# A two-layer hybrid trunk on one core: the order of weight parts in six blocks, the mean ahead of the root, the sines a block later, one last store

## The chip, the cores and the metric

The kernel runs on one core of one Trainium2 chip. The metric is the device time of that core in microseconds (us). Three timed runs of the kernel before gave 876.5, 876.67 and 876.76 us; their median, 876.67, is the time that is compared. The trace comes from one more execution, which took 876.84 us.

## What is computed

Two layers act on a stream `x` of 256 tokens by 1024 features, in float32; then comes a final RMSNorm. In words of the reference:

```python
def hybrid_layer(x, ...):
    h = rmsnorm(x, norm_mix)
    cb, cc, cu, q, k, v, g, ga, gb = jnp.split(h @ w_in, ...)
    y_conv = short_conv_mixer(cb, cc, cu, conv_w, w_conv_out)          # gated width-3 convolution
    y_ret = retention_mixer(q, k, v, g, positions, ret_norm, w_ret_out)  # rotary q, k; 4 heads
    x = x + (sigmoid(ga) * y_conv + sigmoid(gb) * y_ret) @ w_o
    h2 = rmsnorm(x, norm_mlp)
    return x + square(relu(h2 @ w_up)) @ w_down                        # 1024 -> 4096 -> 1024
```

The weights, some 80 million bytes a layer, are read once from device memory.

## The kernel before

**Numbers in two parts.** A float32 weight is not multiplied as such. ACT rounds it to fp32r (the high part) and DVE subtracts that from the weight (the low part): `split`, lines 104 to 106. Activations are split in the same way. A product is then taken from three of the four part products: high weight with high and low activation, low weight with high activation.

**Blocks.** The weights lie in memory as 152 blocks of 1024 x 256 numbers (76 a layer), each loaded in two halves by SP's queue into `raw` (five half buffers) and split into `parts` (three block buffers). A block of `proj` has 16 steps (8 tiles of the contraction by 2 output tiles). Before the change each step is two matmuls with weights of their own: the high part against both parts of the activation (512 columns), then the low part against the high activation (256 columns). So a block is 32 matmuls, with a weight load for each. Blocks 0 to 3 of a layer (the values `v`) and the last down projection go another way, with the tokens as the stationary side and 512 columns in every matmul.

**The order.** There is no scheduler: every engine runs its instructions in the order in which the Python code writes them. `window` counts the blocks (`cnt`). For block i it first writes the work that was put off with `at(n, fn, ph=...)` (n blocks later; `ph` -1, 0, 1 and 2 stand before, between and after the two halves' splits), with the splits of block i + 2 among it, then the matmuls of block i, then the load of block i + 3, then small products (`products_at`). A block's result leaves PSUM in `collect`: ACT copies one half, DVE adds the other.

**The names that the steps below touch.** In layer 0, `proj` blocks 4 and 5 are the first two of the gate `g`; in each layer blocks 23 and 24 of the layer's 76 (23 and 24, 99 and 100 counted over both) are the last of `g` and the first of `ga`. Around these, `mix_values` (tile `o_ps`) and `head_sums` (`var_ps`) put small products between the blocks. `norm_total` sums the squares of x over the features on PE (`mix_st`, right after block 5 in layer 0), `factors_begin` makes the factor `rr` = 1/sqrt(mean + eps) from it: `rsqrt_begin` (ACT's first guess into `rr`, DVE's mean into `rs_m`), then two steps of `newton` in the next two windows. POOL needs `rr` for the gates. `sines` (ACT) takes the rotary angles' sines, and `rotation_tables` (POOL) makes `sin_t` and `cos_t` of them, which DVE multiplies by `rr` (`cosr`, `sinr`).

**The end.** The last tokens' second half of the output is scaled by DVE in two pieces of 256 columns, each stored from SP's queue, while ACT scales and stores the first half.

Of the kernel before, what the change touches and what calls it, by code (L numbers as in the profile page):

```python
# [16 lines left out]
ALU = mybir.AluOpType  # L17
# [4 lines left out]
KT = D // P  # L22
# [3 lines left out]
EPS = 1e-6  # L26
# [8 lines left out]
def _conv(i):  # L35
    return [(n, o + 256 * i) for n, o in (("cc", 1024), ("cu", 2048), ("cb", 0))]


IN_ORDER = (
    [("g", G0), ("g", G0 + 256)]  # L40
    + _conv(0)
    + [e for qk, c in zip((("q", Q0), ("q", Q0 + 256), ("k", K0)), _conv(1)) for e in (qk, c)]
    + [("k", K0 + 256)]
    + _conv(2) + _conv(3)
    + [("g", G0 + 512), ("g", G0 + 768)]
    + [("ga", GA0 + 256 * i) for i in range(4)]
    + [("gb", GB0 + 256 * i) for i in range(4)]
# [6 lines left out]
def trunk_kernel(ctx, tc, px, pos, w, mask, gf, out):  # L54
    nc = tc.nc
# [28 lines left out]
    def stile(name):  # L84
        return s8.tile([P, KT, T], F32, tag="s8", name=name)

    class Parts:
# [5 lines left out]
        def at(self, k):  # L93
            return self.tiles[k // (KT // 2)][:, k % (KT // 2)]
# [33 lines left out]
    cnt = [0]  # L128
    work, small_products, amid = {}, {}, {}
# [5 lines left out]
    def products_at(n, fn, *args):  # L135
        small_products.setdefault(cnt[0] + n, []).append((fn, args))
# [16 lines left out]
    def window(products):  # L153
        i = cnt[0]
        todo = work.setdefault(i, [])

        def run(ph):

            for e in todo:
                if e[0] == ph:  # L160
                    e[1](*e[2])

        run(-1)
        if i in EAGER:
            split_half(i + 2, 0)
        run(0)
        if i > 2 and i not in EAGER:
            split_half(i + 2, 0)
        run(1)
        if i > 2:  # L170
            split_half(i + 2, 1)
        run(2)
        products(blocks[i])
        load_block(i + 3)
        raws.pop(i), blocks.pop(i)
        for fn, args in small_products.pop(i, []):
            fn(*args)
        cnt[0] += 1

    def mm(o, a, b, start, stop):  # L180
        nc.tensor.matmul(o, lhsT=a, rhs=b, start=start, stop=stop, skip_group_check=True)  # L181

    def proj(act, n_blocks=1):

        ps = ps_main.tile([P, 2, 2, T], F32, tag="mm", name="ps")

        def products(blk, b):  # L190
            for k in range(KT):
                a = act[b].at(k)
                for j in range(2):
                    first, end = b == 0 and k == 0, b == n_blocks - 1 and k == KT - 1
                    mm(ps[:, j], blk[:, 0, 2 * k + j, :], a, first, False)
                    mm(ps[:, j, 1], blk[:, 1, 2 * k + j, :], a[:, 0], False, end)
                    for fn, args in amid.pop((cnt[0], 2 * k + j), []):
                        fn(*args)

        for b in range(n_blocks):  # L200
            window(lambda blk: products(blk, b))
        return ps
# [28 lines left out]
    def collect(ps, t=None):  # L231

        t = t2("sum", "sum", 4) if t is None else t
        nc.scalar.copy(t, ps[:, :, 1, :])  # L234
        nc.vector.tensor_tensor(out=t, in0=ps[:, :, 0, :], in1=t, op=ALU.add)  # L235
        return t
# [6 lines left out]

    def rsqrt_begin(y, m, v, scale):

        nc.scalar.activation(y, v, AF.Abs_reciprocal_sqrt, scale=scale, bias=eps)
        nc.vector.tensor_scalar(out=m, in0=v, scalar1=scale, scalar2=EPS, op0=ALU.mult, op1=ALU.add)

    def column_sums(o, hi, lo):

# [45 lines left out]
    def gains(layer, at, n=KT):  # L296
        o = layer * PER_LAYER + at
        return par_sb[:, o:o + n]
# [39 lines left out]
    for n in range(2):  # L338
        c = slice(4 * n, 4 * n + 4)
# [9 lines left out]
    def first_parts(norm=norm):  # L349

        def parts(i, *ks):
            for n, k in enumerate(ks):
                norm.split(k)
                split_half(i, n)

        at(0, parts, 1, 2, 3)
        at(1, parts, 2, 4, 5)
        at(2, parts, 3, 6, 7)
        at(3, norm.split, 0)
        for i, half in ((4, 0), (4, 1)):  # L360
            at(3, split_half, i, half)
        for p in range(NPAIR):
            at(3 if p < 3 else 4, norm.square, p)
        at(4, norm.fold)
        at(5, norm.split_sum)
# [37 lines left out]
    for layer in range(DEPTH):  # L403
        act = [norm.act]
# [3 lines left out]
        def factors_begin(norm=norm):  # L408
            rs_m, rs_a = (tmp.tile([P, T], F32, tag="tmp1", bufs=7, name=n) for n in ("rs_m", "rs_a"))
            rsqrt_begin(rr, rs_m, norm.total_ps, 1.0 / D)  # L410
            at(1, newton, rr, rs_a, rs_m, ph=-1)
            at(2, factors_end, rs_m, rs_a, ph=-1)
# [17 lines left out]
        if layer == 0:  # L430
            first_parts()
            at(0, reduce_angles)
            at(5, sines, ph=2)
            at(6, rotation_tables)
            at(9, nc.sync.dma_start, mask_sb, mask)
        if layer == 0:
            products_at(5, norm_total)
# [73 lines left out]
        def conv_u(p, ps_u, z):  # L511
            t = collect(ps_u)
            nc.gpsimd.tensor_tensor(out=z, in0=z, in1=both(rr2), op=ALU.mult)
            nc.gpsimd.tensor_tensor(out=z, in0=t, in1=z, op=ALU.mult)
            at(1, conv_in, p, z)
# [80 lines left out]
        def head_out(h, rs):  # L596
# [4 lines left out]
            nc.gpsimd.tensor_tensor(out=y, in0=y, in1=both(rs), op=ALU.mult)  # L601
            at(1, split, y, *yr.pair(h))

        hg = small.tile([P, KT], F32, tag="hg", bufs=2, name="hg")
        nc.gpsimd.tensor_scalar(out=hg, in0=gains(layer, G_RET), scalar1=0.5, scalar2=None, op0=ALU.mult)
        v_ps = proj_tokens(act[0], xs if layer == 0 else None)
# [5 lines left out]
        for name, _ in IN_ORDER:  # L612
            n = seen[name] = seen.get(name, -1) + 1
            if name == "q" and n == 0:
                qk = stile("qk")
                q_parts = s8.tile([P, 2, HEADS, T], F32R, tag="s8", name="q_parts")
                k0_parts = s4.tile([P, 2, HEADS, P], F32R, tag="s4", name="k0_parts")
            elif name == "cc" and n == 0:
                yc = Parts("yc")
            elif name == "cc" and n == 2:  # L620
                sc0_parts = s8.tile([P, 2, HEADS, T], F32R, tag="s8", name="sc0_parts")
                sc1 = s4.tile([P, HEADS, P], F32, tag="s2", bufs=1, name="sc1")
                for h in range(HEADS):
                    products_at(1 + h, scores, h)
            elif name == "g" and n == 2:
                osq = s8.tile([P, 2, HEADS, T], F32R, tag="s8", name="osq")
                for h, later in enumerate((0, 0, 1, 2)):
                    products_at(later, mix_values, h)
                products_at(2, head_sums, 0)
                products_at(4, head_sums, 1)  # L630
            elif name == "ga" and n == 0:
                ta = stile("ta")
            elif name == "gb" and n == 0:
                tb = stile("tb")
            ps = proj(act)
            if name == "q":
                at(0, rotate, n, ps)
                if n == 1:
                    at(1, rotations_of_k, ph=1)
            elif name == "k":  # L640
                at(0, rotate, n + 2, ps)
            elif name == "g":
                at(0, gate, n, ps, 3 if n < 2 else 0)
            elif name == "cc":
                at(0, lambda ps: new("z", collect(ps)), ps)
            elif name == "cu":
                at(0, lambda n, ps: conv_u(n, ps, kept["z"]), n, ps)
            elif name == "cb":
                at(0, conv_b, n, ps)
            elif name == "ga":  # L650
                at(0, merge_gate, ta, n, ps)
            elif name == "gb":
                at(0, merge_gate, tb, n, ps)
# [30 lines left out]
        for p in range(NPAIR):  # L684
            at(0, merge_conv, p, proj([yc]))
        mg = Parts("mg")
        for p in range(NPAIR):
            at(0, merge_ret if p < NPAIR - 1 else merge_last, p, proj([yr]))
# [70 lines left out]
    ps = [[both_ps[:, c] for c in HALVES], [third[:, HALVES[0]], ps_misc.tile([P, 512], F32, tag="misc", name="ps")]]  # L759
# [53 lines left out]
    def scaled(j, n, c, r):  # L813

        f = slice(512 * n + c.start, 512 * n + c.stop)
        nc.vector.scalar_tensor_tensor(
            out=o[j][:, f], in0=ps[j][n][:, c], scalar=r, in1=gain[:, f], op0=ALU.mult, op1=ALU.mult
        )
        nc.sync.dma_start(out=out[tok[j], f], in_=o[j][:, f])
# [19 lines left out]
    c = HALVES[0]  # L839
# [2 lines left out]
    nc.vector.tensor_tensor(out=o[1][:, c], in0=ps[1][0], in1=gain[:, c], op=ALU.mult)  # L842
    squares(1, 1)
    r = root(1)
    for n in range(2):
        scaled(1, 1, slice(256 * n, 256 * n + 256), r)
    nc.scalar.activation(o[1][:, c], o[1][:, c], AF.Copy, scale=r)
    nc.scalar.dma_start(out=out[tok[1], c], in_=o[1][:, c])

# [73 lines left out]
```

## Time and profile before

| what | value |
|---|---|
| median of three runs | 876.67 us |
| the profiled execution | 876.84 us |
| its span, first to last instruction | 875.0 us |
| time outside the span | 1.84 us |
| PE busy | 866.8 us, 99% |
| PE's weight loads busy | 754.1 us, 86% |
| DVE, ACT, POOL busy | 680.2, 529.5, 308.4 us |
| granted TensorE clock | 0.999 of the full 2.4 GHz |

The span is cut by what PE does: its matmuls follow one another from 1 us to the last 6 us. A matmul's duration in the trace runs on into the next one's, so the rate of PE is read from start to start, or from stretches of the chain of waits, not from the mean of one. What the other engines do counts where PE waits for it, and in the last 6 us.

### The profile page before, as it was taken

To read this page: it belongs to the slowest core of one execution; us is meant where nothing else is said; L and a number is where in the kernel's file an instruction comes from. 1 tells how busy PE (TensorE), PEld (TensorE's weight loads), DVE (VectorE), ACT (ScalarE), POOL (GpSimd) and SP (SyncE) were. 2 spreads that over 40 slices of the span, in tenths; PEclk is the share of its full clock that TensorE was granted. 3 is DMA by queue.
4 is the path that set the end of the run, shared out by engine and by line. 5 is a ranking of instruction groups with operands and counts; after the bars stand their busy time and mean duration, and the time that the engine had idled before them with its cause. 6 is when DMAs were issued, how large, how long until landed. Compare 5 with 4: busy or idle time off the path is not lost.

```text
span 875.0 us, 12663 instructions
## 1 busy us (share of the span) xinstructions
PE 866.8 (99%) x4846; PEld 754.1 (86%) x4846; DVE 680.2 (78%) x739; ACT 529.5 (61%) x761; POOL 308.4 (35%) x191
## 2 busy tenths in 40 slices
PE   9999999999999999999999999999999999999997
PEld 6888888888888888888888888888888888888885
DVE  5799899999898766555567989999979896663443
ACT  6766665956467777444447665578645587772333
POOL 3857755361213222000013587455411322240000
PEclk9999999999999999999999999999999999999999
DMA  9746455556655655555554555545565565565541
GB/s 329 231 170 208 138 194 183 168 174 226 202 194 170 216 187 193 196 188 187 178 199 167 183 172 195 171 158 187 185 210 175 194 198 189 191 218 171 196 137 48
DMA packets 45996, 163.53 MB, mean 187 GB/s; under 512 B 5104, under 2 KB 5744, under 8 KB 45936
## 3 DMA queue, kind: packets, MB, share of 16 engines
q1 hardware_dynamic: 45648, 162.29, 55.4%
q8 instruction: 38, 0.62, 0.3%
q10 hardware_dynamic: 288, 0.44, 0.2%
q14 instruction: 22, 0.18, 0.1%
HBM read 161.66 MB, written 1.05 MB: 186 GB/s over the span
## 4 chain that ended last, share of the span: by engine, by line
PE 87%; POOL 5%; DVE 4%; DMA 1%; ACT 1%; issue 1%; SPq 0%; DVEq 0%; POOLq 0%
PE ps L181 85%; DVE parts L106 2%; PE o_ps L181 1%; DMA pos_i<-pos 1%; POOL red L371 1%; POOL ang L386 1%; DMA raw<-w 1%; POOL mix_sum L281 1%; POOL rot L458 1%; POOL qk L459 0%; DVE sum L235 0%; PE sc_ps L181 0%; ACT parts L105 0%; POOL qk L451 0%; POOL acc L534 0%
## 5 line engine op out<-in xcount | busy, mean ns | idle before, releaser
L106 DVE TENSOR_TENSOR parts<-raw,parts 128x1024 fp32r<-128x1024 f32 (+1 forms) x304 | 436.7, 1474 | 94.2 <-ACT parts L105 93.8
L105 ACT CAST parts<-raw 128x1024 fp32r<-128x1024 f32 (+1 forms) x304 | 304.5, 1049 | 110.8 <-PE ps L181 79.8
L181 PE MATMUL ps<-mix,parts 128*128 128x512 f32 (+1 forms) x1792 | 316.1, 337 | 1.0 <-DVE parts L106 1.0
L181 PEld LDWEIGHTS ps<-mix,parts 128*128 128x128 f32 x1792 | 274.0, 188 | 38.9 <-DVE parts L106 1.6
L181 PE MATMUL ps<-mlp,parts 128*128 128x512 f32 (+1 forms) x1024 | 178.1, 336 | 0.0
L181 PEld LDWEIGHTS ps<-mlp,parts 128*128 128x128 f32 x1024 | 156.5, 188 | 20.9
L730 POOL TENSOR_TENSOR u<-u,rr2m 128x512 f32<-128x512 f32 x32 | 46.5, 1454 | 126.2 <-ACT u L729 113.1
L235 DVE TENSOR_TENSOR sum<-ps,sum 128x512 f32<-128x512 f32 x78 | 53.3, 684 | 47.4 <-ACT sum L234 47.3
L181 PE MATMUL ps<-up,parts 128*128 128x512 f32 (+1 forms) x512 | 88.9, 336 | 0.0
L181 PE MATMUL ps<-parts,up 128*128 128x512 f32 x384 | 87.5, 389 | 0.0
L181 PEld LDWEIGHTS ps<-up,parts 128*128 128x128 f32 x512 | 78.3, 188 | 10.5
L181 PEld LDWEIGHTS ps<-parts,up 128*128 128x128 f32 x384 | 71.9, 188 | 14.9
L234 ACT COPY sum<-ps 128x512 f32<-128x512 f32 x78 | 45.4, 583 | 61.9 <-PE ps L181 61.7
L181 PE MATMUL ps<-yr,parts 128*128 128x512 f32 (+1 forms) x256 | 44.7, 336 | 0.0
L181 PE MATMUL ps<-mg,parts 128*128 128x512 f32 (+1 forms) x256 | 44.7, 336 | 0.0
L181 PE MATMUL ps<-yc,parts 128*128 128x512 f32 (+1 forms) x256 | 44.7, 336 | 0.0
L181 PEld LDWEIGHTS ps<-yc,parts 128*128 128x128 f32 x256 | 39.1, 188 | 5.2
L181 PEld LDWEIGHTS ps<-yr,parts 128*128 128x128 f32 x256 | 39.1, 188 | 5.2
L181 PEld LDWEIGHTS ps<-mg,parts 128*128 128x128 f32 x256 | 39.1, 188 | 5.2
L181 PE MATMUL ps<-parts,mix 128*128 128x512 f32 x180 | 41.6, 392 | 0.0
L181 PEld LDWEIGHTS ps<-parts,mix 128*128 128x128 f32 x180 | 33.7, 188 | 7.5 <-ACT parts L105 0.6
L281 POOL TENSOR_TENSOR mix_sum<-mix_sum,sq 128x512 f32<-128x512 f32 x6 | 9.9, 1644 | 83.4 <-ACT sq L279 83.2
(166 smaller groups left out, 747.5 us busy)
## 6 DMA issues: line engine op xcount, KB each, us to landing
raw<-w SPq DMA_DIRECT2D x302, 512.0 KB, 4.0
raw<-w SPq DMA_DIRECT2D x4, 256.0 KB, 5.0
px_sb<-px SPq DMA_DIRECT2D x3, 256.0 KB, 7.3
mask_sb<-mask SPq DMA_DIRECT2D x1, 512.0 KB, 7.6
gain<-gf SPq DMA_DIRECT2D x1, 512.0 KB, 4.5
out<-o SPq DMA_DIRECT2D x2, 256.0 KB, 2.1
out<-o SPq DMA_DIRECT2D x2, 128.0 KB, 2.0
out<-o ACTq DMA_DIRECT2D x1, 256.0 KB, 2.2
```

Of the source, the lines that this page charges most:

```text
L105: nc.scalar.copy(hi, src)
L106: nc.vector.tensor_tensor(out=lo, in0=src, in1=hi.bitcast(F32), op=ALU.subtract)
L181: nc.tensor.matmul(o, lhsT=a, rhs=b, start=start, stop=stop, skip_group_check=True)
L234: nc.scalar.copy(t, ps[:, :, 1, :])
L235: nc.vector.tensor_tensor(out=t, in0=ps[:, :, 0, :], in1=t, op=ALU.add)
L281: nc.gpsimd.tensor_tensor(out=self.sum, in0=self.sum, in1=sq, op=ALU.add)
L371: nc.gpsimd.tensor_scalar(out=out, in0=x_, scalar1=c0, op0=ALU.mult, **ops)
L386: nc.gpsimd.tensor_tensor(out=ang, in0=ang, in1=red, op=ALU.subtract)
L458: nc.gpsimd.tensor_tensor(out=w_, in0=w_, in1=both(sinr), op=ALU.mult)
L730: nc.gpsimd.tensor_tensor(out=u, in0=u, in1=both(rr2), op=ALU.mult)
```

## The change

Four edits. (1) `proj` gets a flag `apart`: with it a block's 16 high matmuls come first, all in a row, and then its 16 low ones; blocks 4 and 5 of layer 0 and blocks 23 and 24 of both layers have it. The sums are the same, in another order. (2) In `rsqrt_begin` DVE's mean is written ahead of ACT's root; both read the same PSUM tile, and the second of them waits for the first. It is used once a layer for the norm and twice a layer for the heads. (3) `sines` moves from window 5 to window 6 (still behind the splits), `rotation_tables` from 6 to 7. (4) The last 512 columns are scaled and stored in one piece.

```diff
-    def proj(act, n_blocks=1):
+    def proj(act, n_blocks=1, apart=False):
...
         def products(blk, b):
-            for k in range(KT):
-                a = act[b].at(k)
-                for j in range(2):
-                    first, end = b == 0 and k == 0, b == n_blocks - 1 and k == KT - 1
-                    mm(ps[:, j], blk[:, 0, 2 * k + j, :], a, first, False)
-                    mm(ps[:, j, 1], blk[:, 1, 2 * k + j, :], a[:, 0], False, end)
...
+            kj = [(k, j) for k in range(KT) for j in range(2)]
+
+            def high(k, j):
+                mm(ps[:, j], blk[:, 0, 2 * k + j, :], act[b].at(k), b == 0 and k == 0, False)
+
+            def low(k, j):
+                mm(ps[:, j, 1], blk[:, 1, 2 * k + j, :], act[b].at(k)[:, 0], False, b == n_blocks - 1 and k == KT - 1)
+
+            if apart:
+                for e in kj:
+                    high(*e)
+                for e in kj:
+                    low(*e)
+                return
...
     def rsqrt_begin(y, m, v, scale):
+        nc.vector.tensor_scalar(out=m, in0=v, scalar1=scale, scalar2=EPS, op0=ALU.mult, op1=ALU.add)
         nc.scalar.activation(y, v, AF.Abs_reciprocal_sqrt, scale=scale, bias=eps)
-        nc.vector.tensor_scalar(out=m, in0=v, scalar1=scale, scalar2=EPS, op0=ALU.mult, op1=ALU.add)
...
-            at(5, sines, ph=2)
-            at(6, rotation_tables)
+            at(6, sines, ph=2)
+            at(7, rotation_tables)
...
+        PER, APART = len(IN_ORDER) + 4 + 12 + 32, (23, 24) + ((4, 5) if layer == 0 else ())
...
-            ps = proj(act)
+            ps = proj(act, apart=cnt[0] % PER in APART)
...
-    for n in range(2):
-        scaled(1, 1, slice(256 * n, 256 * n + 256), r)
+    scaled(1, 1, c, r)
```

On PE, from the end of layer 0's value blocks into block 4, before (`mix_103` and `mix_104` hold the parts of the normed x, `parts` the weights'):

```order
L181 MATMUL ps<-parts,mix_104 128x512 x48
L181 MATMUL ps<-mix_103,parts 128x512
L181 MATMUL ps<-mix_103,parts 128x256
L181 MATMUL ps<-mix_103,parts 128x512
L181 MATMUL ps<-mix_103,parts 128x256
```

The same place after, through blocks 4 and 5 to the column sums:

```order
L181 MATMUL ps<-parts,mix_104 128x512 x48
L181 MATMUL ps<-mix_103,parts 128x512 x8
L181 MATMUL ps<-mix_104,parts 128x512 x8
L181 MATMUL ps<-mix_103,parts 128x256 x8
L181 MATMUL ps<-mix_104,parts 128x256 x8
L181 MATMUL ps<-mix_103,parts 128x512 x8
L181 MATMUL ps<-mix_104,parts 128x512 x8
L181 MATMUL ps<-mix_103,parts 128x256 x8
L181 MATMUL ps<-mix_104,parts 128x256 x8
L181 MATMUL mix_st<-mix_sh,ones 128x256
```

The alternation of 512 and 256 columns has become runs of 16 and 16.

On ACT, behind the last split of window 5 in layer 0, before (`sh` and `turns` are the sines, `rr` the first guess of the root, `rs_a` the square in the Newton step):

```order
L105 CAST parts<-raw 128x1024 [waits DMAHW7_49]
L391 ACT_TABLE_LOAD
L391 ACTIVATE sh<-ang 128x256
L392 ACTIVATE turns<-ang 128x256
L393 ACTIVATE turns<-turns,quarter_turn 128x256 [waits Activation_49]
L246 ACT_TABLE_LOAD
L246 ACTIVATE rr<-mix_st,eps 128x256 [waits PE_49]
L481 ACTIVATE v_parts<-vt,mu 128x256 [waits DVE_49]
```

and after:

```order
L105 CAST parts<-raw 128x1024 [waits DMAHW7_49]
L258 ACT_TABLE_LOAD
L258 ACTIVATE rr<-mix_st,eps 128x256 [waits DVE_49]
L492 ACTIVATE v_parts<-vt,mu 128x256 [waits Activation_49] x2
L245 COPY sg<-ps 128x512 [waits PE_49]
L105 CAST parts<-raw 128x1024 [waits DMAHW0_49]
L105 CAST parts<-raw 128x1024 [waits DMAHW1_49]
L402 ACT_TABLE_LOAD
L402 ACTIVATE sh<-ang 128x256
L403 ACTIVATE turns<-ang 128x256
L404 ACTIVATE turns<-turns,quarter_turn 128x256 [waits Activation_49]
L251 ACTIVATE rs_a<-rr 128x256
```

The three sines and their table load have moved from ahead of the root to behind the next two casts, ahead of the first Newton square; the root now waits for DVE instead of PE.

On DVE at the same place, before:

```order
L106 TENSOR_TENSOR parts<-raw,parts 128x1024 [waits DMAHW7_49,Activation_49]
L247 TENSOR_SCALAR rs_m<-mix_st 128x256 [waits Activation_49]
L487 SCALAR_TENSOR_TENSOR v_parts<-vt,mu,v_parts 128x256 [waits Activation_49] x2
L235 TENSOR_TENSOR sg<-ps,sg 128x512 [waits PE_49,Activation_49]
L106 TENSOR_TENSOR parts<-raw,parts 128x1024 [waits DMAHW0_49,Activation_49]
```

and after:

```order
L106 TENSOR_TENSOR parts<-raw,parts 128x1024 [waits DMAHW7_49,Activation_49]
L257 TENSOR_SCALAR rs_m<-mix_st 128x256 [waits PE_49]
L498 SCALAR_TENSOR_TENSOR v_parts<-vt,mu,v_parts 128x256 [waits DVE_49,Activation_49]
L498 SCALAR_TENSOR_TENSOR v_parts<-vt,mu,v_parts 128x256 [waits Activation_49]
L246 TENSOR_TENSOR sg<-ps,sg 128x512 [waits Activation_49]
```

No row has moved on DVE here; the mean `rs_m` waits for PE's sums instead of ACT's root.

## Rows read from the trace of the kernel before

**Rows 1.** The page: span, then busy time and share of PE and its loads.
```profile
span 875.0 us, 12663 instructions
PE 866.8 (99%) x4846; PEld 754.1 (86%) x4846; DVE 680.2 (78%) x739; ACT 529.5 (61%) x761; POOL 308.4 (35%) x191
```

**Rows 2.** Chain that ended last, in order of time: start, us, engine, tile, instructions.
```profile
126.31 11.10 PE ps L181 x64
...
139.72 5.66 PE ps L181 x32
...
569.48 5.66 PE ps L181 x32
```

**Rows 3.** Timeline of PE, 27 to 40 us: start, us, operation, count.
```profile
27.56 11.45 PE L181 MATMUL ps<-mix,parts 128*128 128x512 f32 x64
38.85 0.28 PE L181 MATMUL mix_st<-mix_sh,ones 128*128 128x256 f32 x1
38.97 0.29 PE L181 MATMUL mix_st<-mix_sl,ones 128*128 128x256 f32 x1
```

**Rows 4.** Groups by form: count, busy us, mean ns of one.
```profile
L181 PE MATMUL ps<-parts,up 128*128 128x512 f32 x384 | 87.5, 389 | 0.0
L181 PEld LDWEIGHTS ps<-yc,parts 128*128 128x128 f32 x256 | 39.1, 188 | 5.2
```

**Rows 5.** Timeline of PE, 859 to 872 us, matmuls of 512 columns alone.
```profile
858.78 10.36 PE L181 MATMUL ps<-parts,up 128*128 128x512 f32 x45
```

**Rows 6.** Timeline of PE, 94 to 120 us: the two waits; in brackets, idle time and releaser.
```profile
95.60 3.74 PE L181 MATMUL ps<-mix,parts 128*128 128x256 f32 x20 [0.64 <-DVE parts L106]
...
107.89 5.59 PE L181 MATMUL ps<-mix,parts 128*128 128x256 f32 x31 [0.34 <-DVE parts L106]
```

**Rows 7.** Timeline of ACT, 39 to 48 us.
```profile
39.99 1.28 ACT L391 ACT_TABLE_LOAD   x1
...
42.57 1.28 ACT L246 ACT_TABLE_LOAD   x1
43.87 0.47 ACT L246 ACTIVATE rr<-mix_st,eps 128x256 f32<-128x256 f32 x1
...
47.41 0.41 ACT L240 ACTIVATE rs_a<-rr 128x256 f32<-128x256 f32 x1
```

**Rows 8.** Timeline of DVE, 40 to 58 us.
```profile
40.01 1.23 DVE L106 TENSOR_TENSOR parts<-raw,parts 128x1024 fp32r<-128x1024 f32 x1 [0.21 <-ACT parts L105]
44.38 0.42 DVE L247 TENSOR_SCALAR rs_m<-mix_st 128x256 f32<-128x256 f32 x1 [3.14 <-ACT rr L246]
...
46.59 2.58 DVE L106 TENSOR_TENSOR parts<-raw,parts 128x1024 fp32r<-128x1024 f32 x2 [0.19 <-ACT parts L105]
49.09 0.41 DVE L241 SCALAR_TENSOR_TENSOR rs_a<-rs_a,rs_m 128x256 f32<-128x256 f32 x1
...
56.24 1.51 DVE L424 TENSOR_TENSOR cosr<-cos_t,rr 128x256 f32<-128x256 f32 x1
```

**Rows 9.** Timeline of POOL, 42 to 58 us.
```profile
42.64 0.74 POOL L397 TENSOR_TENSOR sin_t<-sh,turns 128x256 f32<-128x256 f32 x1 [3.26 <-ACT turns L393]
...
44.37 0.61 POOL L400 TENSOR_TENSOR cos_t<-sh 128x256 f32<-128x256 f32 x1
45.08 0.45 POOL L371 TENSOR_SCALAR cos_t<-cos_t 128x256 f32<-128x256 f32 x1
45.51 3.03 POOL L482 TENSOR_SCALAR v<-vt,mu 128x256 f32<-128x256 f32 x2
...
55.20 2.27 POOL L513 TENSOR_TENSOR sum<-sum,rr 128x512 f32<-128x512 f32 x1
```

**Rows 10.** Timeline of the end: DVE's scaling, first tokens, last tokens, then SP's stores.
```profile
866.09 1.41 DVE L816 SCALAR_TENSOR_TENSOR o<-ps,fin_r,gain 128x512 f32<-128x512 f32 x2
...
870.88 0.88 DVE L816 SCALAR_TENSOR_TENSOR o<-ps,fin_r,gain 128x256 f32<-128x256 f32 x2
871.39 0.81 SPq L819 DMA_DIRECT2D out<-o  x2
```

More of the change, by code (lines that the diff above doesn't have):

```diff
@@ L181, in mm @@
         nc.tensor.matmul(o, lhsT=a, rhs=b, start=start, stop=stop, skip_group_check=True)
-    def proj(act, n_blocks=1):
+    def proj(act, n_blocks=1, apart=False):
         ps = ps_main.tile([P, 2, 2, T], F32, tag="mm", name="ps")
         def products(blk, b):
-            for k in range(KT):
-                a = act[b].at(k)
-                for j in range(2):
-                    first, end = b == 0 and k == 0, b == n_blocks - 1 and k == KT - 1
-                    mm(ps[:, j], blk[:, 0, 2 * k + j, :], a, first, False)
-                    mm(ps[:, j, 1], blk[:, 1, 2 * k + j, :], a[:, 0], False, end)
-                    for fn, args in amid.pop((cnt[0], 2 * k + j), []):
-                        fn(*args)
+            kj = [(k, j) for k in range(KT) for j in range(2)]
[9 more added lines that the diff above has]
+                return
+            for n, e in enumerate(kj):
+                high(*e)
+                low(*e)
+                for fn, args in amid.pop((cnt[0], n), []):
+                    fn(*args)
         for b in range(n_blocks):
```

## The prediction

> **What bounds the kernel now.** The page's head comes first [rows 1]: PE is busy for 866.8 of 875.0 us, so the time is the length of PE's stream plus some 6 us behind it. A busy PE is not yet a fast one, so I read next how fast the stream runs, in the chain of waits [rows 2]. Two ordinary blocks (64 instructions) take 11.10 us, 5.55 each, but the blocks at 139.72 and 569.48 take 5.66, and each has a second such block right behind it; these are blocks 23, 24, 99 and 100. The timeline shows a third pair [rows 3]: blocks 4 and 5 take 38.85 - 27.56 = 11.29 us, 0.19 more than two ordinary ones. They are the six blocks that get the new order, and PE waits for nothing in them.
>
> Next I looked for places where PE does wait. There are two, both on DVE's low parts [rows 6], in blocks 16 and 18 of layer 0, each behind the first high matmul of the block. The bracket counts from the modelled end of a matmul. A matmul of 512 columns is shown as 389 ns [rows 4], but starts follow one another at (10.36 - 0.389) / 44 = 0.2266 us [rows 5]. So the waits are longer than the brackets: at 95.60 it is 0.64 + 0.39 - 0.23 = 0.80 us. At 107.89 the matmul before also paid for a change from plain fp32, and some 0.5 us are left. With 0.1 for the slow start behind each, PE loses about 1.5 us to DVE there. Behind 108 us PE waits for nobody. Up to there DVE's pace, not PE's, sets when block 18 runs.
>
> **The four late blocks (23, 24, 99, 100).** No product is removed: 16 of 512 and 16 of 256 columns stay, with their 32 weight loads. Cost apart: the highs run as the uniform 512-column stream does, 16 x 0.2266 = 3.63 us. For the lows the nearest rows are the column sums, 256 columns each, 0.12 us from start to start [rows 3], so 16 x 0.12 = 1.92. Together 5.55, against 5.66: 0.11 us gained a block, **0.43 for the four**. It equals the ordinary block, which is no accident: there a pair takes 5.55 / 16 = 0.347, just 0.227 + 0.12. So I read the 5.66 as a beat between the two lengths that alternate, which a uniform run can't have. Bounds: if a 256-column matmul took half of 0.2266, a block would be 5.44 and the gain 0.87; if the slowness comes with what stands around these blocks and not from the alternation, it is 0. I take 0.43, by the nearest row. Here nothing hides or swallows it: the whole chain behind 108 us is PE. Low parts are wanted later than before and high parts earlier, but none is waited for in these blocks.
>
> **Blocks 4 and 5.** By the same sum 11.29 - 2 x 5.55 = 0.19 us less on PE. Costed at **nothing**: PE then only waits longer at blocks 16 and 18, until DVE is there. If DVE's part below came early by over 1.5 us, these 0.19 would count as well.
>
> **Mean ahead of the root, sines a block on (layer 0).** What counts is how much earlier DVE reaches block 18. Before, ACT goes from 39.99 through a table load and the sines (to 42.57, 2.58 us) and a second table load, and only then to the root at 43.87 [rows 7]; DVE, free at 41.24, waits 3.14 us for it to take the mean [rows 8]. After, DVE takes the mean at 41.26 (PE's sums were there at 39.3 [rows 3]) and is done at 41.68; ACT's load ends at 41.27, so the root waits 0.4 and starts at 41.7, 2.15 earlier. The values, the gate's sum and two parts behind the mean on DVE, done at 49.17 before [rows 8], come 2 us earlier. But the next step on DVE, the first Newton step, needs ACT's square, and ahead of that ACT now has the table load and the sines. ACT's work is the same as before in another order plus the wait of 0.45, so the square moves from 47.41 to 47.86, done at 48.27. DVE can start the step at 48.31 instead of 49.09: 0.78 us earlier. The rest of the 2 us has turned into a wait of DVE for ACT.
>
> Of these 0.78, POOL takes some back. Its four table operations, before at 42.64 to 45.53 while DVE waited [rows 9], now start when the sines are done, at 47.9, and end at 50.8, beside DVE's Newton step and splits. What that costs is seen elsewhere: while POOL ran a two-input operation of 2.27 us from 55.20, DVE's `cosr` took 1.51 us at 56.24 [rows 8, 9] for 256 columns, where the equally wide Newton step takes 0.41. While POOL ran the two one-input operations on `v`, the two splits at 46.59 took 2.58, two times 1.29 against 1.23 at 40.01: nearly nothing, and POOL itself was the slower. The tables hold two two-input operations, 0.74 and 0.61 us; DVE meets the last third of the first and most of the second: 0.25 + 0.25, so 0.5 us. The Trainium skill says more (SBUF — State Buffer, "SBUF: two separate sides"): a DVE instruction with two SBUF inputs and a GpSimd one that reads SBUF lock each other out for a whole instruction. `cosr` agrees, the splits beside POOL's one-input work at 45.51 don't. By that page all of the tables' 2.9 us would stand against DVE.
>
> So DVE is 0.78 - 0.5 = **0.3 us** early. From there to block 18 it is DVE, POOL and ACT in turn, none of them held by PE: ACT collects a block's result more than a block behind PE. So I carry the 0.3 through; PE is ready by then (it loses 1.5 there). Bounds: 0.8 if POOL takes nothing back, -1.6 if all that POOL does from 48.31 to 50.8 (2.4 us) stops DVE.
>
> The same edit of `rsqrt_begin` in the heads and in layer 1 lets ACT wait for a mean on DVE, 0.42 us for 256 columns [rows 8] and some twice that for the heads' 512. Behind ACT are the collect and the casts of the next blocks; PE waits for none of these behind 108 us, so it costs nothing. Without that cover it would be 0.4 to 0.8 us a place, five places.
>
> **The last store.** One operation of 512 columns takes 1.41 / 2 = 0.71 us against 0.88 for the two [rows 10], so DVE is done at 871.6 instead of 871.76. SP issues once instead of twice: its last issue ends at about 872.05 instead of 872.20. The last transfer is twice as long in exchange. I take **0.1 us** gained, between 0.3 and a loss of 0.1.
>
> **Sum.** 0.43 + 0 + 0.3 + 0.1 = 0.83. The profiled execution took 876.84 (span 875.0 and 1.84 around it) and would take 876.0. It lies 0.17 over the median of 876.67, so I forecast **875.8 us**.
>
> **The rivals.**
> *The slow beat isn't the alternation.* Then the six blocks stay at 5.66 and only 0.4 is left: 876.3. For it: all of them stand behind something irregular (the 512-column stream, `o_ps`). Against: PE waits for no engine in them, and both uniform runs keep their pace.
> *DVE comes late (the tables collide).* DVE loses 2.4 instead of 0.5: 0.78 - 2.4 = -1.6, PE's wait at block 18 grows by that, and the sum is +1.6 - 0.43 - 0.1: 877.7. It turns the sum into a loss when POOL's share passes 1.3 us. Against it are the splits beside `v`. The Trainium skill's rule on the shared lock, above, would give this case.
> *PE's two waits vanish.* If DVE keeps the full 0.8, and parts behind it fall better between POOL's operations so that it grows to the 1.5 that PE loses there, 1.5 + 0.19 + 0.43 + 0.1 = 2.2: 874.5. For it: the root itself is 2.15 earlier. Against: the first square is 0.45 later.
> *The weight loads come out (slower).* A load is 188 ns [rows 4]. In a run of lows each has only a 256-column matmul of 0.12 to hide behind; if loads in such a run couldn't overlap, a low would take 0.19 and a block 1.1 us more. Four blocks are 4.4 us; of the 2.2 of blocks 4 and 5 PE's waits cover 1.5. With the store's 0.1 that is +5.0, 881.7 us. The gain of a block is gone when a low takes 0.127, and the sum turns into a loss at some 0.133. The Trainium skill's rule would bring this (TensorE: Matmul & The Clock Gate, Part 3: Packing small matmuls, "The mechanism"): a weight load overlaps a running matmul only when their row groups differ, and here each takes all rows. Against it is the trace: with 188 ns of load each, 512-column matmuls start every 0.227, and the two column sums 0.12 apart, so loads and matmuls do overlap.
>
> **How the numbers follow.** Forecast as summed: 0.65. Slow beat stays: 0.13. DVE late: 0.1. Waits vanish: 0.07. Loads exposed: 0.05. A measurement of this kernel can tell about 0.2% from no change, which is 1.75 us: 874.9 to 878.4. Forecast, slow beat and late DVE lie inside, 0.88. Vanished waits lie below (0.07), and so does 0.01 of the forecast, whose terms may all stand at their good ends (0.87 + 0.8 + 0.3): 0.08 faster, 0.87 the same, and 0.05, the exposed loads, slower. The range leaves out the loads, the vanished waits and most of the late DVE: 874.8 to 876.8.
>
> **What would show it.** Right: six blocks at 5.55 us, lows 0.12 apart; DVE's wait of 3.14 gone and a wait of about 1.5 for ACT's square ahead of the first Newton step; PE's waits at blocks 16 and 18 shorter by 0.3 together; one issue on SP at 871. Wrong: lows at 0.13 or more; DVE's splits at 49 to 52 us stretched beyond 1.3 each; a wait of PE behind 108 us.

## The result and the profile after

The changed kernel takes 882.83 us (median of 7 runs, 878.07 to 883.32) against 876.76 for the kernel before (seven runs now): a ratio of **1.0057, 95% interval 1.004 to 1.0073**. It is slower by some 6 us; 875.8 was forecast. The profiled execution took 882.83 too, so it speaks for the median.

The page of the changed kernel, head and the stores of the output (count, size, median us to landing):

```profile
span 881.0 us, 12653 instructions
PE 873.7 (99%) x4846; PEld 755.2 (86%) x4846; DVE 681.1 (77%) x738; ACT 529.1 (60%) x761; POOL 302.5 (34%) x191
...
out<-o SPq DMA_DIRECT2D x3, 256.0 KB, 2.1
...
out<-o ACTq DMA_DIRECT2D x1, 256.0 KB, 2.9
```

and, of the kernel before, the two last pieces and ACT's store:

```profile
out<-o SPq DMA_DIRECT2D x2, 128.0 KB, 2.0
out<-o ACTq DMA_DIRECT2D x1, 256.0 KB, 2.2
```

Against [rows 1] the span is 6.0 us longer, and PE is *busy* 6.9 us longer with the same 4846 matmuls. So most of the lost time isn't waiting; PE does the same work more slowly. Where, the chain of waits says, in order of time (start, us, engine, tile, instructions), of the changed kernel:

```profile
39.23 67.83 PE ps L181 x384
...
107.64 5.91 PE ps L181 x32
...
126.59 11.30 PE ps L181 x64
...
140.22 5.57 PE ps L181 x32
...
146.96 5.59 PE ps L181 x32
...
165.29 0.56 PE var_ps L181 x2
165.86 107.41 PE ps L181 x608
...
273.49 192.08 PE ps L181 x1060
```

and the same chain of the kernel before, from the second head sums (`var_ps`) on:

```profile
164.93 0.46 PE var_ps L181 x2
165.39 105.40 PE ps L181 x608
...
271.02 188.89 PE ps L181 x1060
```

PE is 0.47 us late at block 27 (165.86 against 165.39). The two long rows, blocks 27 to 75, with no wait in them, then take 2.01 and 3.19 us longer: **5.2 us over 49 blocks, 0.106 us a block**. (The second row also holds the first 100 matmuls of layer 1, all of 512 columns; they take the same time in both.) The first row is 19 blocks of 16 pairs (512 and 256 columns): 105.40 us make 346.7 ns a pair in the kernel before, 107.41 make 353.3 here, and 16 x 6.6 ns is the 0.106. Read from start to start in ns, matmul by matmul, the quick pace has two patterns (230 and 117; or 230, 113, 232, 118); the slow one repeats over three pairs: 232 and 118, 240 and 120, 236 and 114. The granted clock, 0.999 before and 0.998 after, is the same full level.

The slow pace begins twice. The first time is at block 6: the row at 39.23 is blocks 6 to 17, 5.65 each, and 126.59 shows 11.30 for two blocks, against 11.10 in [rows 2]. Most of that first stretch is hidden: what PE loses up to blocks 16 and 18 it would otherwise have spent there waiting for DVE [rows 6], and at 114 us the lag is 0.06 us. Blocks 19 to 22 show it: +0.44. The second time is at block 27, behind the second head sums. Timeline of the changed kernel there, all engines:

```profile
157.93 0.87 DVE L581 SCALAR_TENSOR_TENSOR sg<-o_ps,hg,sg 128x256 f32<-128x256 f32 x2
158.72 0.68 DVE L257 TENSOR_SCALAR rm<-var_ps 128x512 f32<-128x512 f32 x1
159.43 0.69 ACT L258 ACTIVATE rm<-var_ps,eps 128x512 f32<-128x512 f32 x1 [1.74 <-DVE rm L257]
...
162.38 0.41 ACT L105 CAST osq<-osq 128x256 fp32r<-128x256 f32 x1
164.89 0.41 DVE L106 TENSOR_TENSOR osq<-osq 128x256 fp32r<-128x256 f32 x1
...
165.13 0.72 PE L181 MATMUL var_ps<-osq,ones 128*128 128x512 f32 x2
165.36 0.19 PEld L181 LDWEIGHTS var_ps<-osq,ones 128*128 128x128 f32 x1 [0.15 <-DVE osq L106]
```

and of the kernel before, the same instructions:

```profile
158.05 0.69 ACT L246 ACTIVATE rm<-var_ps,eps 128x512 f32<-128x512 f32 x1
161.00 0.41 ACT L105 CAST osq<-osq 128x256 fp32r<-128x256 f32 x1
163.63 0.41 DVE L106 TENSOR_TENSOR osq<-osq 128x256 fp32r<-128x256 f32 x1
...
164.77 0.62 PE L181 MATMUL var_ps<-osq,ones 128*128 128x512 f32 x2
```

ACT's root now waits 1.74 us for DVE's mean, which stands behind the gate's values on DVE. The last head's squares (`osq`) are behind that root on ACT and 1.4 and 1.3 us later (162.38 for 161.00, 164.89 for 163.63). PE's second load of the head sums waits 0.15 us for them, 0.10 of it from start to start. Behind that, the pace is slow until layer 1.

The rest is the end. ACT's last square of the output, here and then in the kernel before:

```profile
874.70 0.60 ACT L806 ACTIVATE sq<-ps 128x512 f32<-128x512 f32 x1 [2.03 <-PE ps L181]
...
869.18 0.60 ACT L793 ACTIVATE sq<-ps 128x512 f32<-128x512 f32 x1 [2.03 <-PE ps L181]
```

From there to the span's end it is 6.3 us here and 5.8 before. So 5.5 of the 6.0 us come from PE's stream and 0.5 from the last store.

### The profile page after: what moved, and what is told of

It reads as the page before. It is cut to its first block, busy times and chain, and to the rows that moved or that the text cites. A ratio compares the mean times of both kernels' runs of the same rounds, so it can differ in the third digit from the quotient of the medians.

```text
span 881.0 us, 12653 instructions
## 1 busy us (share of the span) xinstructions
PE 873.7 (99%) x4846; PEld 755.2 (86%) x4846; DVE 681.1 (77%) x738; ACT 529.1 (60%) x761; POOL 302.5 (34%) x191
## 4 chain that ended last, share of the span: by engine, by line
PE 99%; DVE 0%; issue 0%; ACT 0%; POOL 0%; POOLq 0%
PE ps L181 97%; PE o_ps L181 1%; PE sc_ps L181 1%; PE warm L355 0%; PE var_ps L181 0%; DVE o L829 0%; PE mix_st L181 0%; PE mlp_st L181 0%; ACT fin_r L814 0%; DVE fin_a L817 0%; ACT sq L806 0%; POOL idle L315 0%; DVE fin_r L816 0%; DVE fin_r L818 0%; POOL ones_f L356 0%
## 5 line engine op out<-in xcount | busy, mean ns | idle before, releaser
L181 PE MATMUL ps<-mix,parts 128*128 128x256 f32 (+1 forms) x1792 | 317.6, 338 | 0.0
L181 PE MATMUL ps<-mlp,parts 128*128 128x512 f32 (+1 forms) x1024 | 179.9, 338 | 0.0
```

## The experiments

The first four runs take the change apart: the new order alone, all but the new order, all but the mean's place, and the new order everywhere. Each ratio is taken against runs of the kernel before in the same round, with medians from 876.74 to 877.12 us.

```diff
 e1: the kernel before, with the new `proj` and
-            ps = proj(act)
+            ps = proj(act, apart=cnt[0] % PER in APART)
 e2: the changed kernel, with
-            ps = proj(act, apart=cnt[0] % PER in APART)
+            ps = proj(act)
 e3: the changed kernel, with
-        nc.vector.tensor_scalar(out=m, in0=v, scalar1=scale, ...)
         nc.scalar.activation(y, v, AF.Abs_reciprocal_sqrt, scale=scale, bias=eps)
+        nc.vector.tensor_scalar(out=m, in0=v, scalar1=scale, ...)
 e4: the kernel before, with the new `proj` and
+    def proj(act, n_blocks=1, apart=True):
 ...
+                    for fn, args in amid.pop((cnt[0], n), []):   # behind each high
+                        fn(*args)
```

> The kernel before with the new order in the six blocks alone (mean, sines and store as before). In the trace of the changed kernel ordinary blocks run at 353 ns a pair instead of 347 in two long stretches: blocks 6 to 22, behind blocks 4 and 5, and blocks 27 to 75, behind a wait of 0.15 us of PE for the heads' squares (DVE) at the second head sums. Theory A: the second stretch is set off by that wait, and the wait comes from the mean ahead of the root (ACT's root waits 1.7 us behind DVE's queue, so the heads' squares come 1.3 us late). Then here blocks 27 to 75 run at 347, blocks 6 to 22 still slow (most of it inside the waits at blocks 16 and 18), and the time is 876.5 to 877.2. Rival B: the new order in blocks 23 and 24 itself sets the second stretch off; then it is slow here too and the time is 881 to 883.

Measured: 876.97 us, ratio 1.0 (0.9991 to 1.0009). Blocks 6 to 22 have the slow pace, blocks 27 to 75 do not. The new order alone costs nothing in sum, and isn't the 5.2.

> The changed kernel without the new order: mean ahead of the root, sines a block on, one last store. Theory A: the heads' squares are late as in the changed kernel, PE waits some 0.1 us at the second head sums, blocks 27 to 75 run at 353: 881 to 883; blocks 6 to 22 at 347. If PE, without the 0.36 us more of the blocks before it, is there when the squares are, or the wait differs, it may fall either way from run to run. Rival B: blocks 27 to 75 at 347, and the time 876 to 877.

Measured: 881.0 us, ratio 1.0053 (1.0037 to 1.007); executions of 877.69, 880.87, 881.12 and 883.54. The loss is there without the new order. The profile fell on the 877.69, where the second head sums did not wait and blocks 27 to 75 were quick. So whether PE meets the late squares seems to differ from execution to execution of one program. That may also be behind the 878.07 among the runs of the changed kernel; no trace of a long execution of e2 or of that short one shows it.

> The changed kernel with the mean behind the root again (order, sines and store as changed). Theory A: no wait at the second head sums, blocks 27 to 75 at 347, blocks 6 to 22 slow: 876.5 to 877.8 (the sines a block on let the root come earlier by itself). Rival B: 881 to 883. If only the sums of the norm and not those of the heads mattered, blocks 27 to 75 would be slow here as well.

Measured: 876.66 us, ratio 0.9999 (0.999 to 1.0009). The loss goes with the mean's place. Its span is 874.9 us. Its chain behind the second head sums:

```profile
164.86 105.40 PE ps L181 x608
...
270.50 188.89 PE ps L181 x1060
```

and its last square on ACT's timeline:

```profile
868.52 0.60 ACT L806 ACTIVATE sq<-ps 128x512 f32<-128x512 f32 x1 [2.03 <-PE ps L181]
```

Both long rows are back at their length of before, and PE's end is 0.66 us earlier than before (868.52 for 869.18). But the tail from that square to the span's end is 6.3 us as in the changed kernel; with two stores it is 5.8 again (e8). So it is in all 17 traces: 6.3 us in the six with one last store, 5.8 to 5.9 in the eleven with two. One last store costs some 0.5 us.

> The kernel before with the new order in every block that alternates (132 of 152), nothing else. If a run of equal matmuls has no second pace (0.2266 and 0.1200 us from start to start in the changed kernel's six blocks), no block can be slow, whatever it comes behind: 5.547 us each; and low parts are wanted 3.6 us into a block, so PE's waits at blocks 16 and 18 (1.5 us) go. Theory: 876.7 - 0.6 (the six) - 1.5 = 874.3 to 875.5. Rival: the long stretches of the changed kernel come from the order as such (a state of PE that 256-column runs bring), then it is 878 or more.

Measured: 881.39 us, ratio 1.0048 (1.0033 to 1.0063): slower, no gain. The slow pace doesn't occur, but an ordinary block in the new order takes 72.35 / 13 = 5.565 (chain), not 5.547, and new waits stand in it. The chain from block 27 on:

```profile
164.93 72.35 PE ps L181 x416
```

and the table of PE's waits (us in total, times, longest):

```profile
PE ps L181 <- DVE mg L697: 1.9, 2, 1.0
...
PE o_ps L181 <- DVE sg L583: 0.3, 1, 0.3
```

A run of highs reads all of an activation in two thirds of the time, so what splits it late is waited for. The low matmuls do start 0.120 us apart, but the first highs behind them take 233, 236, 228, 233 and 231 ns instead of 227. Neither theory had these two costs: the time lies in the rival's range, but not by the rival's cause.

Next, the mean's place at its two uses, and the wait itself:

```diff
 e5: the changed kernel, with
-                products_at(4, head_sums, 1)
+                products_at(5, head_sums, 1)
 e6, e7: the kernel before, with
+    def rsqrt_begin(y, m, v, scale, ahead=False):   # mean first if ahead
 ...
 e6 (heads):
+            rsqrt_begin(rs, rm[:, 1, h, :], st, 1.0 / T, True)
 e7 (norms):
+            rsqrt_begin(rr, rs_m, norm.total_ps, 1.0 / D, True)
```

> The changed kernel with the second head sums one block later (behind block 27 of a layer instead of 26), so that their squares are long there when PE comes; the mean stays ahead, so the squares are as late as before. Theory A (a wait of PE at the second head sums sets the slow stretch off): no wait, blocks 28 to 75 at 347 ns a pair, 877.2 to 878.2, the same in every run. Rival C: the late roots or the mean itself slow what follows (DVE's and ACT's order, not the wait); then the stretch stays and the time is 881 to 883.

Measured: 877.58 us, ratio 1.0005 (0.9995 to 1.0015). The squares are as late as before the edit, but PE no longer meets them. DVE's split on the timeline:

```profile
165.10 0.41 DVE L106 TENSOR_TENSOR osq<-osq 128x256 fp32r<-128x256 f32 x1
```

and the chain:

```profile
154.09 16.65 PE ps L181 x96
170.75 0.46 PE var_ps L181 x2
171.21 99.85 PE ps L181 x576
```

The sums take 0.46 as before the change, and 18 blocks take 99.85 / 18 = 5.55 us. One small product put a block later gives back the 5.2 us.

> The kernel before with the mean ahead of the root for the heads alone (the norm's mean, order, sines and store as before). Theory A: ACT's root waits behind DVE's queue, the squares of the last head are 1.3 us late, PE waits in some executions: 877 in the good ones, 881 to 883 in the others, as the run without the new order gave 877.7 to 883.5. Rival: the heads are innocent and it is 876.7 in all runs.

Measured: 882.02 us, ratio 1.0054 (1.0039 to 1.0069). The loss is there with this edit alone, 4.9 us against 877.12 in the same runs. PE's timeline at the second product of the head sums:

```profile
166.20 0.50 PE L181 MATMUL var_ps<-osq,ones 128*128 128x512 f32 x1 [0.57 <-DVE osq L106]
```

But its chain behind that is not the changed kernel's:

```profile
166.70 105.39 PE ps L181 x608
272.09 0.23 PE mlp_st L181 x2
272.32 192.07 PE ps L181 x1060
```

PE waits longer (0.57), the pace behind the wait is quick, and it turns slow only behind the two column sums `mlp_st`, where nothing waits. In this trace the slow pace costs 3.2 us and the wait 0.8 (the sums take 1.29 us from start to start, before 0.46). So a wait need not end in the slow pace, and the slow pace need not begin at a wait.

> The kernel before with the mean ahead of the root for the norms alone. Sines stay where they were, so ACT's root is as late as before and DVE gains its 3.1 us of idle only for a 0.4 us instruction. Theory A: no slow stretch, 876.4 to 877.0 in all runs. Rival: the norm's mean is what sets the stretch off, 881 to 883.

Measured: 877.02 us, ratio 0.9994 (0.9984 to 1.0003). The mean's place at the norms costs nothing.

Then the parts that might be left as a gain: the order and the sines without the other two edits (e8), and on that the new order in other blocks.

```diff
 e8: the changed kernel with e3's edit and two last stores
 e9: e8, with
-        ... (23, 24) + ((4, 5) if layer == 0 else ())
+        ... (23, 24) + ((16, 17, 18) if layer == 0 else ())
 e10: e9, with e5's edit
 e11: e8, with
+        ... (23, 24)
```

> New order in the six blocks and sines a block on; mean behind the root, two last stores. The run with one store ended PE 0.67 us earlier than the kernel before, but its end behind the last matmul was 6.34 us long instead of 5.87, as in every run with one store. Theory: two stores give the 0.47 back, 876.1 to 876.3. If the longer end belonged to something else than the one store, it stays at 876.6.

Measured: 876.72 us, ratio 0.9997 (0.9988 to 1.0006), above the 876.1 to 876.3 of its theory. The kernel before took 877.12 in the same runs, so it is 0.4 us quicker by the medians, which the interval doesn't tell from nothing; the tail itself is 5.8 us as expected.

> As the run with new order and sines, but the new order in blocks 16, 17, 18, 23 and 24 of layer 0 (not 4 and 5) and 23 and 24 of layer 1. Low parts are then wanted 3.6 us into blocks 16 and 18, so PE need not wait for DVE there, and blocks 6 to 15 keep 347. By the blocks alone PE ends 1.5 us earlier than in that run: 875.2. But the squares of the last head, ready at about 163.8 there, leave PE only 0.8 us of margin at the second head sums; with PE 1.5 us earlier it waits there. Theory A forecasts that this small wait brings the slow stretch back: 880 to 882 in all or some executions. Rival: only the mean ahead has that effect; 875.2.

Measured: 876.09 us, ratio 0.9991 (0.9981 to 1.0001). The slow stretch behind the head sums that it foresaw did not come: the sums did not wait. Most of the 1.5 us that the blocks should have gained didn't come either. PE now waits in `o_ps` for the gate's values, 0.2 us by the bracket and some 0.4 from start to start (block 23 takes 6.03 us, in e8 5.66), and blocks 19 to 22, behind block 18 in the new order, have the slow pace, another 0.4.

> The same with the second head sums one block later, so that no wait stands at the head of the long row of ordinary blocks. Theory A: 875.0 to 875.8, lower than the kernel before in every execution. Rival: 880 or more if the stretch is set off by something else, or 876.7 if PE's gain at blocks 16 to 18 is lost in waits for DVE behind.

Measured: 876.2 us, ratio 0.9994 (0.9985 to 1.0003), between its theory and its rival. The trace has the wait of e9 for the gate's values (0.3 by the bracket) and the slow blocks 19 to 22 again.

> As the run with new order and sines, but with blocks 4 and 5 in the old order (23 and 24 of both layers in the new). Theory A: behind interleaved blocks 4 and 5 the column sums leave blocks 6 to 15 at 347 as in the kernel before, so PE comes to block 16 some 1 us earlier and waits there for DVE; behind it everything is as in that run: 876.2 to 876.9, no change. If blocks 4 and 5 in the new order were a gain, it would be 0.2 more, if the slow blocks 6 to 22 behind them were a loss on the path, up to 1 less.

Measured: 876.19 us, ratio 0.9992 (0.9983 to 1.0002). e9 to e11 are the quickest versions, some 0.7 us under the kernel before (876.85 in the same runs) by their medians; the intervals of the ratios still hold 1.

The last runs ask what brings the slow pace. First, late squares without the mean's edit:

```diff
 e12: the kernel before, with
-            at(1, split, sq[:, 0, :], osq[:, 0, h, :], osq[:, 1, h, :])
+            at(1, split, ..., ph=1 if h == 3 and layer == 0 else 0)
```

> The kernel before with one split moved: the last head's squares of layer 0 are split behind the next collect and the first of the next block's casts, some 3.7 us later (ACT at 164.7 instead of 161.0), so that PE waits some 0.5 us for them at the second head sums. No root, mean, order, sine or store is changed. Theory A (a wait of PE at that place is enough): blocks of layer 0 behind it run at 353 ns a pair in a long row, at once or from the next column sums (271 us) on as in the run with the mean ahead for the heads alone; 879.5 to 883. Rival: the wait is only a companion of the mean ahead of the root; then the wait costs itself and the time is 877.0 to 877.5.

Measured: 882.76 us (879.53 to 884.78), ratio 1.0069 (1.0045 to 1.0092). PE's wait was 1.75 us, far more than meant, and the profiled execution (881.22) had the quick pace behind it, 188.86 us in the second long row. Two executions were 2 to 5 us longer than the others and may have had the slow pace, but no trace shows them. It settles nothing.

So I took an irregularity at which nothing can wait: one block, 28, 50, or 28 of the kernel before, in the new order.

```diff
 e13: the changed kernel, with
+        ... ((4, 5, 28) if layer == 0 else ())
 e14: the changed kernel, with
+        ... ((4, 5, 50) if layer == 0 else ())
+            at(0, up_out, p, proj([norm.act], apart=cnt[0] % PER in APART))
 e15: the kernel before, with
+        ... (28,) if layer == 0 else ()
```

> The changed kernel, with block 28 of layer 0 in the new order too: nothing waits there, it is only irregular. The pace is a state of the alternating stream, set by its last irregularity: the slow pace that begins behind the second head sums (block 27, 353.3 ns a pair) can end at block 28, and if the stream lands in one of its two quick patterns there, blocks 29 to 75 run at 5.55 us and the time falls by 47 x 0.107 = 5.0 us, to 877 to 878.5. If it lands in the slow pattern again, nothing moves: 882 to 883.3, and this tells nothing apart. The rival, that the slow pace is kept by something lasting that the late squares leave behind (the other engines and the loads standing later against PE from there on): no reordering of one block takes that away, slow through block 75, 882 to 883.3.

Measured: 882.94 us (882.84 to 883.06), ratio 1.0067 (1.0052 to 1.0082). Blocks 29 to 75 are slow as before the edit.

> The changed kernel, with block 50 of layer 0 (in the up projection) in the new order too. A state of the stream: slow through block 49, and if block 50 puts it into a quick pattern, blocks 51 to 75 gain 25 x 0.107 = 2.7 us, 879.5 to 880.7; so the two runs together would scale with where the irregular block stands. If it stays slow behind, 882 to 883.3. Something lasting: slow through block 75 whatever block 50 does, 882 to 883.3.

Measured: 882.7 us (880.81 to 882.92), ratio 1.006 (1.0045 to 1.0075). Slow up to block 50 and behind it. By themselves these two tell nothing apart, as their expectations said.

> The kernel before, with the new order in block 28 of layer 0 alone. A state of the stream: the quick pattern that the kernel before has from block 27 on may be lost behind an irregular block with no wait at all; if so blocks 29 to 75 run at 353.3 ns a pair and the time rises by 5.0 us, to 881.5; if the stream lands in a quick pattern it stays at 876.5 to 877. If a slow stretch needs a wait, or late squares: 876.5 to 877 in any case.

Measured: 881.99 us (881.83 to 882.26), ratio 1.0056 (1.004 to 1.0073). One block of the kernel before with its 32 matmuls in another order, and the whole is 5.0 us slower by the medians of the same runs (876.95 before). Its span is 880.3 us. The table of PE's waits (us in total, times, longest), without two that lie before 6 us:

```profile
PE ps L181 <- DVE parts L106: 1.0, 2, 0.6
...
```

and its chain:

```profile
165.13 0.46 PE var_ps L181 x2
165.59 107.25 PE ps L181 x608
...
273.08 192.07 PE ps L181 x1060
```

The waits are those of the kernel before (its two in [rows 6], 0.64 and 0.34, are this line). The squares are not late, and the head sums take 0.46 us. Blocks 25 to 27 run at 347 ns a pair; behind block 28 a pair takes 353.3 ns, through block 75: the second long row is 192.07 against 188.89. **The slow pace needs no wait and no late work; something irregular in the stream is enough.** So what keeps the pace slow isn't a lasting effect of late squares on the other engines and loads: here none were late.

## Why the prediction was wrong

**The step that failed: "The same edit of `rsqrt_begin` in the heads and in layer 1 ... costs nothing."** The wait that it feared was too short, 0.4 to 0.8 us a place: the root waits 1.74, since the mean stands behind the gate's values on DVE. And its list of what stands behind the root on ACT was incomplete. It named the collect and the casts of the next blocks; the last head's squares stand there too, and PE reads them less than a microsecond after DVE has split them: in the trace of before the split starts at 163.63 and takes 0.41, and PE's sums start at 164.77, a cover of 0.7 us. They came 1.3 later. Going through the queue by name would have shown a wait of PE of about half a microsecond (e6: 0.57; in the changed kernel 0.15, since PE itself was later by then).

**The second failure was to price a wait, or a reordered block, by its own length.** 0.10 us of delay brought 5.2. The prediction read 5.55 us as *the* length of an ordinary block and 5.66 as a "beat" of six special ones, from rows which showed both. In fact 5.55 and 5.65 are two paces of the same alternating instructions, and the stream keeps the one it has fallen into for tens of blocks. Its line on the six blocks, that the slowness might come "with what stands around these blocks", was nearest to that. None of the rivals had it, and the slower one (exposed weight loads) gave 881.7 by a cause that is not there; that it came near is luck. Two of its signs of being wrong did come: a wait of PE behind 108 us (0.15 at 165), and splits beyond 1.3 us each (2.65 for two, below).

**Blocks in the new order: nearly as forecast, in themselves.** Highs start 0.2267 us apart and lows 0.1200 (forecast 0.2266 and 0.12). Blocks 4 and 5 of the changed kernel on PE's timeline:

```profile
27.73 11.27 PE L181 MATMUL ps<-mix,parts 128*128 128x512 f32 x64
38.83 0.28 PE L181 MATMUL mix_st<-mix_sh,ones 128*128 128x256 f32 x1
```

They take 11.10 us from start to the column sums, 0.19 less than in [rows 3], as forecast. The four late ones were mis-sized: 5.57 and 5.59 us in the chain, not 5.55, so some 0.28 for the four and not 0.43; the rest goes into the slow first highs behind 256-column products. By the Trainium skill (TensorE: Matmul & The Clock Gate, Part 3, "The mechanism") a weight load overlaps running matmuls only where the row groups differ; a load into the background weight buffer, which the same section also lets run ahead, was left out of the rival. By the first rule alone a low would have to take the load's 0.19 us [rows 4]; the measured 0.1200 doesn't agree with that here. What the blocks do to the stream behind them was left out: blocks 4 and 5 bring the slow pace to blocks 6 to 22, some 1.8 us, of which 0.44 is seen.

**DVE's stretch in layer 0: steps right, POOL's share mis-sized.** Timeline of the changed kernel, DVE, with the first of POOL's tables:

```profile
41.30 0.41 DVE L257 TENSOR_SCALAR rs_m<-mix_st 128x256 f32<-128x256 f32 x1
...
48.32 0.76 DVE L252 SCALAR_TENSOR_TENSOR rs_a<-rs_a,rs_m 128x256 f32<-128x256 f32 x1 [1.48 <-ACT rs_a L251]
49.11 0.58 DVE L253 SCALAR_TENSOR_TENSOR rr<-rs_a,rr 128x256 f32<-128x256 f32 x1
...
50.22 2.65 DVE L106 TENSOR_TENSOR parts<-raw,parts 128x1024 fp32r<-128x1024 f32 x2
52.80 0.41 DVE L252 SCALAR_TENSOR_TENSOR rs_a<-rs_a,rs_m 128x256 f32<-128x256 f32 x1
...
48.06 0.73 POOL L408 TENSOR_TENSOR sin_t<-sh,turns 128x256 f32<-128x256 f32 x1 [5.88 <-ACT turns L404]
```

and of the kernel before, the splits and the second Newton step at the same place:

```profile
50.48 2.35 DVE L106 TENSOR_TENSOR parts<-raw,parts 128x1024 fp32r<-128x1024 f32 x2
52.74 0.42 DVE L241 SCALAR_TENSOR_TENSOR rs_a<-rs_a,rs_m 128x256 f32<-128x256 f32 x1
```

The mean at 41.30 (forecast 41.26), the wait of 1.48 for ACT's square (1.5), the step at 48.32 (48.31) and POOL's tables at 48.06 (47.9) came as told. What failed is the size of POOL's share, 0.5 us. Beside POOL's tables the first Newton step takes 0.76 us instead of 0.41 and the two splits behind it 2.65 instead of 2.35, and from the first Newton step to the second it is 4.48 us (48.32 to 52.80) against 3.65 (49.09 to 52.74). So POOL takes back 0.83, and the 0.78 gained is gone by 52.80. It is the same in every trace: 4.48 or 4.49 with the sines a block on, 3.65 or 3.66 without. DVE splits block 18's weights at 105.49, before at 105.52; so the 0.3 us early is not there. (In e3 it is 105.07, but in the six traces with sines and mean of this norm as before the same split starts anywhere from 105.2 to 106.0, so single executions can't tell 0.45 us apart.)

**The last store: wrong sign.** 0.1 us gained was forecast, with a loss of 0.1 as the bound. DVE and SP do finish as counted. But SP's last transfer is now one of 256 KB, and ACT's store of the other half, at the same time, lands in 2.9 us instead of 2.2. The term "twice as long in exchange" had no row behind it; it measured 0.5 us lost.

**The sum.** 5.2 us of pace behind the head sums, 0.44 at blocks 19 to 22, 0.1 of wait, 0.06 up to block 18, 0.5 at the end, less 0.28 in the late blocks: 6.0 us, the difference of the spans.

**What stays open.** Why the alternating stream has these patterns, and which irregularity leads to which. What the traces show: an alternating block right behind a run of lows was slow every time (e13, e14, e15), and so it was with a few small products between (the column sums behind block 5, the scores behind block 18 in e9). Right behind the uniform 512-column stream (blocks 4 and 5 of the kernel before) and behind `o_ps` alone (its blocks 23 and 24) it was slow too: these are the prediction's slow blocks. Behind `o_ps` and `var_ps` together (block 25) it was quick in every trace in which that block alternates, and so it was behind the second `var_ps` without a wait; behind a wait it was either. A few small products without a wait follow no rule: the scores turned a slow stream quick in e3 (block 18) and left it slow in the changed kernel (blocks 19 to 21), and `mlp_st` turned a quick one slow in e6 and left it quick in the kernel before. That the pattern of three pairs repeats through 49 blocks, whatever DVE, ACT and POOL do there, speaks for a state of PE's own stream; no run isolates it.

## What to carry to other kernels

An engine whose stream looks gap-free can still have two paces: compare the length of the same row of the chain in both kernels before looking for waits, and price an edit of such a stream by what runs behind it as well. Before writing one instruction ahead of another engine's, list everything that is queued behind the one that will wait, up to the first thing that the bounding engine reads, and compare the wait with that thing's slack. Where a product's operand has little slack, move the product, not the engines: one block later cost nothing here and gave back 5.2 us.

## What was not expected of the hardware

A stream of 512- and 256-column matmuls, each with its own weight load, runs at 346.7 or 353.3 ns a pair at a granted clock of 0.998 to 0.999, and keeps to one of the two for up to 49 blocks (272 to 277 us); reordering the 32 matmuls of one block is enough to change it, for 5.0 us (e15). The first 512-column matmuls behind a run of 256-column ones take 233, 236, 228, 233 and 231 ns before they settle at 227. Two last stores of 256 KB on two queues at once end 0.5 us later than one of 256 and two of 128 KB.
